# Stores of values in plain patterns, a gathered load, and bias sums queued behind other GpSimd work, in a two-network transformer kernel

## The chip, the cores and the metric

The kernel runs on one core of a Trainium2 chip. Its time is the device time of one execution in microseconds (us); the time of record is the median of several executions. A profiled execution of the same kernel gives the trace from which all rows below are read. The engines are named as the profile names them: PE (TensorE matmul), PEld (its weight load), DVE (VectorE), ACT (ScalarE), POOL (GpSimd) and SP (SyncE, which here only issues DMAs). A name such as SPq or POOLq is the queue of DMAs that this engine issues.

## The reference, cut to what matters

Two networks of two layers each work on 512 tokens of width 1024, in fp32. Each layer of the first network projects its input once and feeds three attention branches:

```
proj = h @ w_in[l]
c_q, c_kv, k_r, qkv_b, qkv_c, gate_logits = jnp.split(proj, IN_SPLITS, axis=-1)
y_a = mla_mixer(c_q, c_kv, k_r, ...)          # latent attention, 8 heads
y_b = dilated_mixer(q_b, k_b, v_b)            # DIL_PATTERNS = ((128,1),(512,4),(2048,16)), 4 heads each
y_c = neighbourhood_mixer(q_c, k_c, v_c, rpb) # 8 heads on an 8 x 64 grid, a learned bias
merged = sum of gates[i] * (y_i @ w_i);  x = x + merged @ w_o;  then a gated feed-forward block
```

The dilated branch splits the 512 tokens into 1, 4 or 16 interleaved sequences and lets each head attend within its own sequence. With dilation 16, token t belongs to sequence t mod 16, and each sequence holds 32 tokens. The neighbourhood branch lets each grid cell attend to a window of 8 x 16 cells, with a bias added to the scores. The second network (attention, short convolution, Fourier mixing) isn't touched by the change.

## The kernel before, in words

Each fp32 product is made as three matmuls of split operands (a high and a low part), so every weight tile is loaded by SP into `wst`, split by ACT into `whi` (line 251) and by DVE into `wlo` (line 252), and used by PE in lines 269 to 271. Tokens are in the columns of most tiles; the values of the dilated and neighbourhood branches are the exception.

`v_tokens` computes these values with tokens in the rows, for 5 units of 4 heads: units 0 and 1 together, then unit 2 (the third dilated group), then units 3 and 4 (the two neighbourhood groups). For each block of 128 tokens (`tk`), ACT and DVE split the product into the tile `vn` (lines 254 and 255, two buffers), and `v_store` sends it by one GpSimd DMA (line 759) to the DRAM tensor `vd` of 512 rows and 2560 columns. Unit 0 and 1 are stored with rows in the order of the tokens. Unit 2 is stored with its rows sorted by sequence (row 32 r + l for token 16 l + r) and units 3 and 4 with theirs sorted by grid column. The sorting is done by the DRAM side of the store: its pattern has an outer level of 8 (unit 2) or 2 (units 3 and 4), a second level of 16 or 64, and rows of 512 columns. `v_load` reads the values back by GpSimd DMAs (line 769) into a tile `V`, one pair of heads at a time, when the unit needs them; for unit 2 that is one DMA of rows in storage order.

`branches` puts the groups of attention heads into one stream: latent attention, three dilated groups, two neighbourhood groups. `attn_pair` handles a pair of heads as steps of three parts: `score` (line 341; a mask or a bias is added by DVE in line 348), `turn` (a transpose by PE in line 365, and its split) and `value` (lines 392 or 406). `stream` issues the score of a step, then the turn of the step before it, then the value of the step before that; dense products fill the spaces between (`weave`). In its last lines `value` adds three parts of the output: ACT copies two, DVE adds (line 416), GpSimd adds the last (line 417).

For a pair of neighbourhood heads, `pre` loads the bias of each of the two heads from DRAM on the GpSimd queue (line 1015) into a tile `bias` (two buffers) and adds the constant mask `maskc` on GpSimd (line 1016). `maskc` is loaded by SP into the space that `krhl` held; `krhl` is last read by the DMAs of line 860. `dil_merge` weights the three dilated groups: it stores statistics by line 516, reads them back (line 963), computes on DVE, stores and reads back factors (lines 979 and 521), and multiplies (line 984, DVE).

The softmax denominators of the other groups go a like way: `inverse` copies a row (line 508, DVE), stores it (line 510), reads it back spread over 64 partitions (line 521), and DVE multiplies by it (line 877).

Nothing fixes the order of instructions on an engine by hand, but for a few places with `issue_after`, which puts an instruction behind a given one on the same engine without a wait on data. A planner orders each engine's instructions as the program is built: it simulates engines and DMAs with its own costs, and takes the foremost instruction of the program that it believes ready. On the chip each engine then works in that order, and an instruction that waits holds all behind it.

Of the kernel before, what the change touches and what calls it, by code (L numbers as in the profile page):

```python
# [11 lines left out]
F32 = mybir.dt.float32  # L12
F32R = mybir.dt.float32r
AF = mybir.ActivationFunctionType
ALU = mybir.AluOpType
# [6 lines left out]
P = 128  # L22
# [192 lines left out]
class _Net:  # L215
# [105 lines left out]
    def attn_pair(self, scores, nk, mask, v, order, rq=None, wide=False, pre=None, post=None, home=None):  # L321
# [5 lines left out]
        nc = self.nc  # L327
# [51 lines left out]
        def value(j, g):  # L379
            rows = slice(64 * j, 64 * j + 64)  # L380
            o = c["o"]
            cost = 0
            if wide:
                if g == 0:
                    c["ob"] = self.bank("O")
                ob = c["ob"]
                if g % 2:
                    qs = slice((g - 1) * P, (g + 1) * P)
                    ph, pl = c.pop(("p", j, g // 2))
                    for x in (ph, pl):  # L390
                        for kt in range(nkt):
                            self.last = nc.tensor.matmul(ob[:, qs], v(j, 0, kt), x[:, kt], start=x is ph and kt == 0,  # L392
                                                         stop=x is pl and kt == nkt - 1)
                            cost += 110
                if g == 3:
                    nc.scalar.activation(o[rows], ob[64:128], AF.Copy)
                    nc.vector.tensor_tensor(o[rows], ob[0:64], o[rows], op=ALU.add)
            else:

                p = c.pop(("p", j, g))  # L400
                for hb in range(per // 2):
                    ob = self.bank("T" if hb else "O")
                    b0 = g * per + 2 * hb
                    for i in range(2):
                        for kt in range(nkt):
                            nc.tensor.matmul(ob[:, i * 256:i * 256 + 256], v(j, b0 + i, kt),
                                             p[:, (2 * hb + i) * nkt + kt].rearrange("p a q -> p (a q)"),
                                             start=kt == 0, stop=kt == nkt - 1)
                            cost += 110
                    dst = self.two_blocks(order(o[rows]), b0)  # L410
                    part = lambda r, x: self.two_parts(ob[r], x, dst)
                    ll = self.t(self.tp, "ll", (P, 256), bufs=2)
                    lo = self.two_blocks(ll[rows], 0, like=dst)
                    nc.scalar.activation(lo, part(slice(0, 64), 1), AF.Copy)
                    nc.scalar.activation(dst, part(slice(64, 128), 0), AF.Copy)
                    nc.vector.tensor_tensor(dst, part(slice(0, 64), 0), dst, op=ALU.add)  # L416
                    nc.gpsimd.tensor_tensor(dst, dst, lo, op=ALU.add)  # L417
            if g == 4 // per - 1 and j == 1 and post:
                c["late"](o)
            return cost  # L420

        steps = [(lambda j=j, g=g: score(j, g), lambda j=j, g=g: turn(j, g), lambda j=j, g=g: value(j, g))
                 for j in range(2) for g in range(4 // per)]
        return [(pre if i == 0 else None, *s) for i, s in enumerate(steps)]
# [297 lines left out]
    def v_tokens(self, win, rc, vd):  # L722

        sl = [slice(tk * P, (tk + 1) * P) for tk in range(4)]
        w = 2560
        at = lambda o, *ap: bass.AP(vd.tensor, vd.offset + o, [list(x) for x in ap])
        ps = [self.bank(x) for x in ("mm", "mm", "mm", "T")]
        for k in range(8):  # L730
            if k % 2 == 0:
                wt = self.weights(win[24 + k // 2])
            o = slice(k % 2 * 512, k % 2 * 512 + 512)
            for tk in range(4):
                self.mm3(ps[tk], self.hh[:, k, sl[tk]], self.hl[:, k, sl[tk]], wt[0][:, o], wt[1][:, o], k == 0, k == 7)
                yield 650
        for tk in range(4):
            self.v_store(ps[tk], rc()[:, tk:tk + 1], vd[sl[tk], 0:1024], "p" + "hl"[tk % 2])
        for u in (2, 3, 4):
            wt = [self.weights(win[24 + 2 * u + c]) for c in range(2)]  # L740
            for tk in range(4):
                if tk % 2 == 0:
                    bk = self.bank("mm")
                ps = bk[:, tk % 2 * 256:tk % 2 * 256 + 256]
                for k in range(8):
                    o = slice(k % 4 * 256, k % 4 * 256 + 256)
                    self.mm3(ps, self.hh[:, k, sl[tk]], self.hl[:, k, sl[tk]], wt[k // 4][0][:, o], wt[k // 4][1][:, o],
                             k == 0, k == 7)
                    yield 330
                dst = at(8 * tk * w + 512 * u, (w, 8), (32 * w, 16), (1, 512)) if u == 2 else \  # L750
                    at(2 * tk * w + 512 * u, (w, 2), (8 * w, 64), (1, 512))
                self.v_store(ps, rc()[:, tk:tk + 1], dst, "vn")
        yield 0

    def v_store(self, ps, scale, dst, tag):
        n = ps.shape[1] // 64
        vn = self.t(self.tp, tag, (P, n, 2, 64), F32R, bufs=2)
        self.split(vn[:, :, 0], vn[:, :, 1], ps.rearrange("p (h d) -> p h d", h=n), scale)
        self.nc.gpsimd.dma_start(out=dst, in_=vn.rearrange("p h x d -> p (h x d)").bitcast(F32))

    def v_load(self, vd, pair, width, parts):

# [9 lines left out]
    def branches(self, l, r, put_r, gates, first_outputs, first_products, load_split, qk_tiles, qc):  # L772
        nc, a = self.nc, self.a
        h = (self.hh, self.hl)
        nat = lambda ap: ap
        win = a["win"][l]
        rows = lambda j: slice(64 * j, 64 * j + 64)

        def const(src, n, name, tag=None):
            c = self.cp.tile([P, n], F32, name=f"{name}{l}", tag=tag or name)  # L780
            nc.sync.dma_start(out=c, in_=src)
            return c


        st = {}
# [86 lines left out]
        def finish(i, order, tap, stay=False):  # L872
            def f(stats):
                rd = self.inverse(stats[:, 1])

                def late(o):
                    nc.vector.tensor_tensor(order(o), order(o), self.blocked(rd, order), op=ALU.mult)
                    self.tap(*tap[:1], o, tap[1])
                    if not stay:
                        self.put_y(i, o)  # L880
                        return
                    x = qk_tiles()
                    self.split(x[:, 0], x[:, 1], o)
                    qc[0].append(x[:, 0])
                    qc[1].append(x[:, 1])
                return late
            return f
# [11 lines left out]
        def unit(u, put, vparts, res):  # L899
            for p in range(2):  # L900
                q, *ks = [qk_tiles() for _ in range(3)]
                t = [q[:, 0], q[:, 1]] + [x[:, i] for i in range(2) for x in ks]
                for side in range(2):
# [6 lines left out]
        orders = (nat, lambda ap: ap.rearrange("p (l r) -> p r l", r=4), lambda ap: ap.rearrange("p (l r) -> p r l", r=16))  # L910
        vparts = ([(0, [(1, P)], (P, 4), 0), (4, [(1, P)], (P, 3), 64)],
                  [(0, [(4, P)], (1, 4), 0)],
                  [(0, [(1, P)], (P, 4), 0)])
        g0tiles = ((0, 1), (4, 5), (5, 6), (2, 3))
        g0keys = (0, 64, 192, 256)
        sd = self.t(self.dr, "sd", (6, 4, S), bufs=1)
# [86 lines left out]
        def nb_groups(u):  # L1003
            if u == 0:
                st["mc"] = const(a["maskC"], 768, "maskc", "krhl")
            groups = []
            for p in range(2):
                t, v = res["C", u][p]
                bias = {}

                def pre(bias=bias, p=p):
                    for j in range(2):
                        bt = self.t(self.tp, "bias", (P, 768), bufs=2)
                        hd = 4 * u + 2 * p + j
                        nc.gpsimd.dma_start(out=bt, in_=a["rpb"][l, hd])
                        nc.gpsimd.tensor_tensor(bt, bt, st["mc"], op=ALU.add)
                        bias[j] = bt
                    return iter(())
                groups += self.attn_pair(
                    self.pair_scores(t, bs, lambda x, b: x[:, 8 * KC0[b]:8 * KC0[b] + 256]), 256,  # L1020
                    lambda j, b, bias=bias: bias[j][:, CTYPE[b] * 256:CTYPE[b] * 256 + 256],
                    lambda j, b, kt, v=v: v[:, g0tiles[b][kt], j * P:(j + 1) * P], blk, pre=pre,
                    post=finish(6 + 2 * u + p, blk, (f"yc{l}", (2 * u + p) * P), u == 1))
            return groups
# [646 lines left out]
```

## Time and profile before

| | us |
|---|---|
| median of 3 runs | 2438.22 (2437.87 to 2441.62) |
| profiled execution, its own time | 2432.9 |
| its span in the trace | 2431.1 |
| PE busy in the span | 2325.6 |
| DVE busy | 1571.2 |
| ACT busy | 1169.5 |
| POOL busy | 695.4 |

The profiled execution took 1.8 us more than its span in the trace, and 5.3 us less than the median of the runs. PE is busy in 96% of the span. The two layers of the first network hold the stages that the change touches: from about 50 to 450 us in the first layer and from about 985 to 1450 us in the second. The granted TensorE clock is 0.984 of full speed over the span.

### The profile page before, as it was taken

How to read it: one execution, taken by the hardware profiler on the slowest of the kernel's cores; microseconds unless marked ns; L12 is line 12 of the kernel's file. 1: busy time of each engine (PE TensorE's matmuls, PEld its weight loads, DVE VectorE, ACT ScalarE, POOL GpSimd, SP SyncE). 2: the span in 40 equal slices, each digit the busy share in tenths (PEclk: the TensorE clock that was granted, in tenths of full speed). 3: DMA queues.
4: the chain of work that ended last, by engine and by line, in shares of the span. 5: the costliest groups of instructions: out<-in, count | busy, mean ns of one | idle time of the engine just before them, and what ended most of it. 6: DMA issues, size and time to landing. Idle time of an engine off the chain costs nothing. (4 is left out here: it accounts for less than half of the span.)

```text
span 2431.1 us, 31714 instructions
## 1 busy us (share of the span) xinstructions
PE 2325.6 (96%) x11356; PEld 1932.1 (79%) x11356; DVE 1571.2 (65%) x2367; ACT 1169.5 (48%) x2064; POOL 695.4 (29%) x745
## 2 busy tenths in 40 slices
PE   8989999989999999989999999999999899979996
PEld 7878887878888888878887877878877788858884
DVE  6768798665443334857788656777333767697666
ACT  5656685434222223646676444323222466435653
POOL 3135456332111001223356423111112121242215
PEclk9999999999999999999999999999999999989998
DMA  5445457555333344544546656876344332324222
GB/s 185 136 152 156 146 165 229 183 183 173 95 96 98 104 130 141 147 142 127 166 138 205 224 162 197 275 257 200 95 133 139 115 96 82 92 77 124 75 82 78
DMA packets 135405, 352.62 MB, mean 145 GB/s; under 512 B 26552, under 2 KB 33944, under 8 KB 135248
## 3 DMA queue, kind: packets, MB, share of 16 engines
q1 hardware_dynamic: 103760, 279.91, 35.9%
q0 software_dynamic: 31488, 70.69, 10.1%
q8 instruction: 89, 1.46, 0.3%
q14 instruction: 68, 0.56, 0.1%
HBM read 281.54 MB, written 41.66 MB: 133 GB/s over the span
## 5 line engine op out<-in xcount | busy, mean ns | idle before, releaser
L251 ACT ACTIVATE whi<-wst 128x1024 fp32r<-128x1024 f32 (+4 forms) x387 | 374.0, 967 | 626.4 <-PE mm L270 187.5
L252 DVE TENSOR_TENSOR wlo<-wst,whi 128x1024 fp32r<-128x1024 f32 (+4 forms) x387 | 471.4, 1219 | 257.4 <-ACT whi L251 256.7
L271 PE MATMUL mm<-hh,wlo 128*128 128x512 f32 x1184 | 467.1, 395 | 8.2 <-DVE wlo L252 8.2
L269 PE MATMUL mm<-hh,whi 128*128 128x512 f32 x1184 | 473.0, 400 | 0.5 <-ACT tmp L538 0.5
L270 PE MATMUL mm<-hl,whi 128*128 128x512 f32 x1184 | 466.6, 394 | 0.0
L271 PEld LDWEIGHTS mm<-hh,wlo 128*128 128x128 f32 x1184 | 223.8, 189 | 55.9 <-DVE wlo L252 9.0
L269 PEld LDWEIGHTS mm<-hh,whi 128*128 128x128 f32 x1184 | 224.2, 189 | 41.0 <-ACT tmp L538 0.7
L270 PEld LDWEIGHTS mm<-hl,whi 128*128 128x128 f32 x1184 | 224.3, 189 | 40.7 <-issue 0.2
L706 POOL TENSOR_TENSOR s<-s,rf 128x512 f32<-128x512 f32 x44 | 75.9, 1726 | 398.0 <-ACT s L705 398.0
L541 POOL DMA_DIRECT2D ry<-tmp x136 | 67.9, 505 | 184.8 <-ACT tmp L538 86.6
L341 PE MATMUL S<-qk,qk 128*128 128x512 f32 (+2 forms) x512 | 108.1, 329 | 12.2 <-ACT E L353 12.2
L365 PE MATMUL T<-ident,E 128*128 128x128 f32 x768 | 117.1, 273 | 1.0 <-ACT E L353 1.0
L251 ACT ACTIVATE ph<-T 128x512 fp32r<-128x512 f32 x160 | 94.6, 595 | 45.5 <-PE T L365 43.8
L365 PEld LDWEIGHTS T<-ident,E 128*128 128x128 f32 x768 | 94.0, 141 | 19.1 <-ACT E L353 1.2
L252 DVE TENSOR_TENSOR pl<-T,ph 128x512 fp32r<-128x512 f32 x128 | 87.2, 683 | 25.6 <-ACT ph L251 25.1
L341 PEld LDWEIGHTS S<-qk,qk 128*128 128x128 f32 x512 | 79.8, 192 | 23.7 <-ACT E L353 14.6
L350 ACT ACTIVATE E<-E,stats 128x256 f32<-128x256 f32 (+1 forms) x160 | 73.0, 457 | 51.9 <-DVE stats L348 51.4
L417 POOL TENSOR_TENSOR O<-O,ll 64x256 f32<-64x256 f32 x72 | 75.1, 1045 | 65.7 <-DVE O L416 61.3
L303 POOL TENSOR_TENSOR tmp<-tmp,tmp 128x512 f32<-128x512 f32 x26 | 41.7, 1603 | 170.5 <-ACT tmp L299 166.6
L269 PE MATMUL S<-hh,whi 128*128 128x512 f32 x208 | 82.3, 395 | 6.0 <-ACT hh L254 6.0
L271 PE MATMUL S<-hh,wlo 128*128 128x512 f32 x208 | 82.0, 394 | 1.5 <-DVE wlo L252 1.5
L270 PE MATMUL S<-hl,whi 128*128 128x512 f32 x208 | 82.1, 395 | 0.0
(649 smaller groups left out, 5491.5 us busy)
## 6 DMA issues: line engine op xcount, KB each, us to landing
wst<-win SPq DMA_DIRECT2D x153, 512.0 KB, 3.8
wst<-w SPq DMA_DIRECT2D x120, 512.0 KB, 3.6
mw<-wada SPq DMA_DIRECT2D x48, 512.0 KB, 4.4
td<-gate SPq DMA_DIRECT2D x48, 256.0 KB, 3.5
V<-vd POOLq DMA_DIRECT2D x20, 512.0 KB, 5.4
qk<-qk POOLq DMA_DIRECT2D x40, 256.0 KB, 4.0
ry<-tmp POOLq DMA_DIRECT2D x136, 64.0 KB, 3.8
wst<-wo SPq DMA_DIRECT2D x16, 512.0 KB, 3.8
```

What stands on the lines that cost most here:

```text
L251: nc.scalar.activation(hi, src, AF.Copy)
L252: nc.vector.tensor_tensor(lo, src, hi.bitcast(F32), op=ALU.subtract)
L269: mm(out, ah, bh, start=start, stop=False, **kw)
L270: mm(out, ah, bl, start=False, stop=False, **kw)
L271: mm(out, al, bh, start=False, stop=stop, **kw)
L303: self.nc.gpsimd.tensor_tensor(new, acc, sq, op=ALU.add)
L341: nc.tensor.matmul(sp[:, i * nk:(i + 1) * nk], a, b, start=n == 0, stop=n == len(ops) - 1)
L350: nc.scalar.activation(e[:, sl], e[:, sl], AF.Exp, scale=-1.0, bias=m, accum_out=d)
L365: nc.tensor.transpose(tp[:, i * P:(i + 1) * P], e[:, i * P:(i + 1) * P], self.ident)
L417: nc.gpsimd.tensor_tensor(dst, dst, lo, op=ALU.add)
L541: nc.gpsimd.dma_start(out=y[r:r + 32], in_=f[r ^ 32:(r ^ 32) + 32])
L706: nc.gpsimd.tensor_tensor(s, s, r, op=ALU.mult)
```

## The change

There are three parts.

1. Stores. `v_store` takes a list of (rows of the tile, DRAM pattern) and issues one DMA for each. Unit 2 is now stored in the order of the tokens (one DMA for 128 rows, as before). For units 3 and 4 each store becomes two, of 64 rows each, with one row stride.
2. Load. Unit 2's `V` is gathered on loading: for each pair of heads four DMAs of 128 rows (4 sequences of 32 tokens each) take the place of one of 512 rows.
3. Bias sums. `value` keeps its last GpSimd addition (line 417) as `self.summed`, and the addition of bias and mask (line 1016) is queued behind the one kept at that point of the program.

```diff
@@ attn_pair, value
-                    nc.gpsimd.tensor_tensor(dst, dst, lo, op=ALU.add)
+                    self.summed = nc.gpsimd.tensor_tensor(dst, dst, lo, op=ALU.add)
@@ v_tokens
-            self.v_store(ps[tk], rc()[:, tk:tk + 1], vd[sl[tk], 0:1024], "p" + "hl"[tk % 2])
+            self.v_store(ps[tk], rc()[:, tk:tk + 1], [(slice(0, P), vd[sl[tk], 0:1024])], "p" + "hl"[tk % 2])
...
-                dst = at(8 * tk * w + 512 * u, (w, 8), (32 * w, 16), (1, 512)) if u == 2 else \
-                    at(2 * tk * w + 512 * u, (w, 2), (8 * w, 64), (1, 512))
+                dst = [(slice(0, P), vd[sl[tk], 1024:1536])] if u == 2 else \
+                    [(slice(64 * i, 64 * i + 64), at((2 * tk + i) * w + 512 * u, (8 * w, 64), (1, 512))) for i in range(2)]
@@ v_store
-        self.nc.gpsimd.dma_start(out=dst, in_=vn.rearrange("p h x d -> p (h x d)").bitcast(F32))
+        for rows, d in dst:
+            self.nc.gpsimd.dma_start(out=d, in_=vn[rows].rearrange("p h x d -> p (h x d)").bitcast(F32))
@@ branches
-                  [(0, [(1, P)], (P, 4), 0)])
+                  [(0, [(1, 4), (16, 32)], (4, 4), 0)])
@@ nb_groups, pre
-                        nc.gpsimd.tensor_tensor(bt, bt, st["mc"], op=ALU.add)
+                        with self.tc.issue_after(self.summed.ins):
+                            nc.gpsimd.tensor_tensor(bt, bt, st["mc"], op=ALU.add)
```

## Rows read from the trace of the kernel before

**Rows 1.** The page: busy us and share of each engine.
```profile
PE 2325.6 (96%) x11356; PEld 1932.1 (79%) x11356; DVE 1571.2 (65%) x2367; ACT 1169.5 (48%) x2064; POOL 695.4 (29%) x745
```

**Rows 2.** Timeline, first layer: start, length, engine, line, operation, idle before and releaser.
```profile
133.05 0.47 DVE L255 SCALAR_TENSOR_TENSOR vn<-mm,rc,vn 128x256 fp32r<-128x256 f32 x1
...
138.00 4.63 POOL L1016 TENSOR_TENSOR bias<-bias,maskc 128x768 f32<-128x768 f32 x2 [9.78 <-DMA maskc<-maskC]
142.59 1.63 POOL L759 DMA_DIRECT2D vd<-vn  x2
...
154.32 0.47 ACT L254 ACTIVATE vn<-mm,rc 128x256 fp32r<-128x256 f32 x1 [9.72 <-DMA vd<-vn]
...
157.21 1.65 PE L341 MATMUL S<-qk,qk 128*128 128x512 f32 x3 [6.58 <-ACT E L353]
```

**Rows 3.** Windows behind two stalls: busy of PE, PEld, DVE, ACT, POOL; PEclk, DMA, GB/s.
```profile
157.20:162.00 4.80, 4.79 (x17) 4.38 (x18) 3.69 (x6) 2.34 (x6) 2.12 (x3) 0.51 0.91 292
...
1090.60:1094.00 3.40, 3.34 (x9) 2.70 (x10) 3.40 (x7) 1.78 (x4) 0.84 (x1) 0.53 0.74 254
```

**Rows 4.** Timeline, second layer, same columns as rows 2.
```profile
1069.54 0.27 DVE L508 COPY row<-T 8x128 f32<-8x128 f32 x1
...
1069.80 3.65 POOL L1016 TENSOR_TENSOR bias<-bias,maskc 128x768 f32<-128x768 f32 x2 [12.95 <-DMA maskc<-maskC]
1073.39 1.67 POOL L759 DMA_DIRECT2D vd<-vn  x2
...
1085.24 1.09 POOL L521 DMA_DIRECT2D RD<-rdd  x2 [9.64 <-DMA rdd<-row]
...
1088.78 0.69 DVE L877 TENSOR_TENSOR O<-O,RD 128x512 f32<-128x512 f32 x1 [10.87 <-DMA RD<-rdd]
...
1090.66 0.80 PE L271 MATMUL mm<-hh,wlo 128*128 128x512 f32 x1 [8.24 <-DVE wlo L252]
```

**Rows 5.** Second layer: two PE waits (timeline), ACT's waits from 980 to 1130.
```profile
1045.30 0.96 PE L341 MATMUL S<-qk,qk 128*128 128x512 f32 x3 [1.23 <-ACT E L353]
...
1053.97 0.39 PE L269 MATMUL mm<-whi,hh 128*128 128x256 f32 x1 [0.73 <-DVE vn L255]
...
ACT vn L254 <- DMA vd<-vn: 8.7, 2, 5.0
```

**Rows 6.** Line 759, units 3 and 4, second layer: issue ns and landing us, min/median/max.
```profile
L759 POOL DMA_DIRECT2D vd<-vn x8: 801/837/852, 1020.8 to 1092.5; - x8
...
DMA to landing us min/median/max: 8.5/10.2/12.5
```

**Rows 7.** Line 759, unit 2, second layer.
```profile
DMA to landing us min/median/max: 4.3/4.6/5.0
```

**Rows 8.** Line 759, units 0 and 1, second layer (512 KB each).
```profile
L759 POOL DMA_DIRECT2D vd<-ph x2: 532/574/617, 989.0 to 990.3; - x2
...
DMA to landing us min/median/max: 3.4/5.5/7.7
```

**Rows 9.** Timeline, first layer, where the neighbourhood group begins.
```profile
343.84 1.70 POOL L417 TENSOR_TENSOR O<-O,ll 64x256 f32<-64x256 f32 x2
344.30 0.41 DVE L348 CUSTOM_DVE_ANT_0 E<-S,bias 128x256 f32<-128x256 f32 x1
...
347.86 0.60 POOL L516 DMA_DIRECT2D sd<-row  x1 [2.32 <-DVE row L515]
```

**Rows 10.** Timeline, first layer, the merge of the dilated groups.
```profile
376.53 0.69 DVE L984 TENSOR_TENSOR o<-o,RD 128x512 f32<-128x512 f32 x1 [4.61 <-DMA RD<-fd]
...
377.76 1.22 PE L406 MATMUL O<-pl,V 128*128 128x256 f32 x4 [3.37 <-DVE O L416]
```

**Rows 11.** First layer: unit 2's first load of values, and the first addition after its use.
```profile
305.12 0.80 POOL L769 DMA_DIRECT2D V<-vd  x1
...
336.41 0.90 POOL L417 TENSOR_TENSOR O<-O,ll 64x256 f32<-64x256 f32 x1 [0.56 <-DVE O L416]
...
L769 POOL DMA_DIRECT2D V<-vd x2: 802/808/814, 305.1 to 327.0; - x2
```

## The prediction, made before the changed kernel was run

> **What bounds the kernel now.** The page comes first: PE is busy for 2325.6 of 2431.1 us [rows 1], so only some 105 us can be won without taking work from PE, and every edit here is worth what it does to PE's idle time and to its clock. Next I asked for busy time and granted clock in stretches of 10 us through the two layers of the first network, to find where PE stands still. Three places lie where values are stored or a bias sum runs; at each, the timelines of POOL, ACT, DVE and PE side by side tell what it waits for.
>
> First place, first layer, 150.6 to 157.2 us. PE waits 6.58 us for an exponential on ACT. ACT is late because its split of the last value tile waits 9.72 us for a free buffer of `vn`, that is for a store of values to land. That store was issued at 142.59, though its tile was complete at 133.5. What held it is the pair of bias sums in front of it on POOL: they waited 9.78 us for the mask to land and then ran 4.63 us [rows 2]. Nothing needs these sums before 344.30 [rows 9]. After the stall PE runs for 4.8 us at a granted clock of 0.51, so near 1.2 instead of 2.4 GHz [rows 3].
>
> Second place, second layer, 1082.4 to 1090.7 us. PE waits 8.24 us for a low weight part. DVE could not make it, since it stood 10.87 us at a multiplication by a denominator that hadn't landed. POOL read it back only at 1085.24, after 9.64 us of waiting for a stored row of 4 KB. That row was ready at 1069.81 and was issued at about 1075.06, behind two bias sums (again held, 12.95 us, by the mask) and two value stores [rows 4]. So the row lost 5.25 us before it was issued and some 10 us in landing, behind two stores that themselves land in about 10 us [rows 6]. The clock stays at 0.53 for 3.4 us after it [rows 3].
>
> Third place, second layer, 1044 to 1054 us: PE waits 1.23 and 0.73 us. ACT waited for `vn` buffers there as well, 8.7 us in two waits [rows 5].
>
> **The stores.** All 128-row stores of `vn` carry 256 KB; only the DRAM pattern differs. With an outer level of 2 (units 3 and 4) they take 8.5 to 12.5 us to land [rows 6], with an outer level of 8 (unit 2) 4.3 to 5.0 [rows 7]. The stores of units 0 and 1, plain rows, land in 3.4 to 7.7 us with twice the bytes [rows 8]. The row stride doesn't explain it, for unit 2's was the longest. So I expect the new halves (64 rows, 128 KB, plain) to land in 3 to 5 us and bound them by 3.4 and 10.2. Unit 2 gains at most a microsecond, on a landing that nobody waits for.
>
> The Trainium skill says the same in "DMA: Bandwidth & Descriptors", section "Why a DMA increments its semaphore by 16 and not by 1": a transfer runs on the largest number of engines, at most 16, that divides the outer counts of both patterns, so 2, then 8, then 16 here; the trace agrees in order (10.2, 4.6 and 5.5 us). It also speaks against a part of the change: the gathered loads have an outer count of 4, so 4 engines each, and if that made them late enough to reach PE by the 10 us worked out below, in one layer, the gain would be 6.8 instead of 16.8 us.
>
> On POOL each store of units 3 and 4 becomes two issues. One cost 0.837 us [rows 6]; a plain one costs 0.574 [rows 8]. That is +0.31 us for each of 16, about 5 us of POOL over the kernel, beside 71% of idle time [rows 1].
>
> **The gathered load.** Four issues of about 0.808 us take the place of one, +2.4 us for each of four loads, 9.7 us of POOL in all [rows 11]. The first load is issued at 305.12, and the addition that follows its use comes at 336.41, so there are about 31 us for it [rows 11]. With an outer count of 4 I bound one gathered DMA by the landings for counts 8 and 2, 4.6 and 10.2 us, at half the bytes of either. Four in a row at 4.6 are 18 us and hidden; four at 10.2 would be 41 us and 10 too late. I take it as hidden, since halving the bytes puts each nearer the lower end.
>
> **The bias sums.** The sums now stand behind the addition of line 417 that was traced last. A score is traced two steps ahead of its value, so for the first neighbourhood pair that is the second addition of the pair issued at 343.84, which ends at 345.54 [rows 9]. POOL no longer stands at 128 or 1057 us, so the value stores and the row go out when they are ready. This has two prices.
>
> One is the mask on DVE: the first use of a bias was at 344.30, and the first sum (1.83 us, half of 3.65 [rows 4]) can end at 347.4 at the earliest, so DVE is held 3.1 us unless the planner puts other work before it. At the merge DVE stood 4.61 us and PE, which stopped 2.47 us later, lost 3.37 [rows 10]. So about 2.5 us of a hold on DVE are free; 3.1 cost 0.6 us a layer, 1.2 in all. For later pairs I count nothing here and leave them to rival (c).
>
> The other is the merge. Its store of statistics stands at 347.86 [rows 9]. With two sums of 1.83 us from 345.54 it goes out at 349.2, 1.35 us late. The merge's end already stops PE for 3.37 us [rows 10], so this passes through: 2.7 us in two layers. The bounds are 0 (the planner lets the store go first) and 3.7 us a layer.
>
> **The sum.** First place: 6.58 us, and 4.8 x (1 - 0.51) = 2.35 us for the clock, 8.9. Second place: 8.24 + 3.4 x (1 - 0.53) = 9.8. Third place: 1.23 + 0.73 = 2.0. Together 20.7 us. Less 1.2 for the masks and 2.7 for the merge it is 16.8. From the profiled execution's 2432.9 us that is 2416.1; this execution lies 5.3 us under the median, so against the median of 2438.22 I predict 2421.
>
> What comes next where the stalls go: at the first place ACT reaches the same order 9.72 us sooner where PE waited 6.58, so 3 us are left [rows 2]. At the second the row would be issued near 1071 behind the same stores, land with them near 1075, be read back by about 1080 (1085.24 to 1088.78 is 3.5 us [rows 4]), and the weight part (1.9 us from 1088.78 to 1090.66) would be ready near 1081, with 1 to 2 us to spare before 1082.4. That is the tightest step.
>
> **Rivals.** (a) The stores land no sooner, because two halves of one tile share what limited the whole. Then only the hold is lifted. The first place still goes (the store is issued 9.1 us earlier, and ACT waited 9.72). At the second, 5.25 of 8.24 us go and the clock stays low. Gain 8.9 + 5.2 less 3.9, or 10.2: 2428. For it: the halves go out together. Against it: rows 6 to 8, where only the outer count differs. The Trainium skill's page "DMA: Bandwidth & Descriptors", section "Rules for kernel authors", holds that two transfers to disjoint partition halves run one after the other; that rule would lean to this case. No row of this trace shows two such halves.
>
> (b) POOL's new order costs more than I took: both sums pass whole into the merge (3.7 us a layer) and the mask's hold whole into PE (3.1). That is 13.6 us of the 20.7: gain 7.1, 2431. For it: the sums stand ahead of the merge in the program, and the planner takes the foremost. Against it: 2.5 us of slack at the merge [rows 10].
>
> (c) Slower. If each of the eight pair starts held DVE for 3.1 us and PE felt all of it, that would be 24.8 us, with 2.7 for the merge 27.5 against 20.7: 2445. It decides once a hold costs PE more than 2.25 us (20.7 - 2.7 over 8), so with under a microsecond of slack on DVE. The merge shows 2.5.
>
> (d) The planner makes the order anew, and the merge's stall (3.37 us and a slow clock after it, about 5 us a layer) goes as well in both layers: 2411.
>
> (e) The change doesn't do what it says: the planner had placed the sums late in its own view and the edge alters nothing. Excluded here, since in the first layer they were issued some 200 us ahead of their first use [rows 2, 9].
>
> **How the numbers follow.** The forecast has 0.60 (its own range 2415 to 2427, from the bounds of the merge and the third place), (a) 0.10, (b) 0.12, (c) 0.06, (d) 0.12. The range from 2411 to 2431 takes in (a), (b) and (d) at their prices and leaves out (c) and the tails. A change within 0.2%, 4.9 us, can't be told from none in this kernel: under 2433.3 is faster, over 2443.1 slower. Part of (b) and the better part of (c) fall inside: faster 0.88, same 0.06, slower 0.06.
>
> **What would show it.** In the changed profile: no bias sum on POOL before about 340 and 1275 us; landings of units 3 and 4 of 3 to 5 us; no wait of ACT for `vn`; PE busy throughout 150 to 160 and 1080 to 1090 at full clock; a hold on DVE of up to 3 us at the first neighbourhood mask; the merge's stall 1 to 2 us longer. Wrong would be: landings that stay near 10 us, or new PE idle time over 5 us a layer from 340 to 430 and from 1275 to 1360 us.

## The result, and the profile after

The changed kernel takes 2409.86 us (median of 4 runs, 2409.14 to 2413.86), the kernel before 2439.86 on the same chip (4 runs, 2437.87 to 2441.62): a ratio of 0.9881, 95% interval 0.9864 to 0.9898, so 25 to 33 us less. I had forecast 2421 in a range of 2411 to 2431. The direction was right; the gain was underestimated, and the time lies just under the range.

The two profiled executions differ by less, 2432.9 against 2413.86 us. The one of before was faster than all 60 runs of that kernel beside the experiments (2434.05 to 2449.39), and the one of after the slowest of its four. With a second profile of either (runs e4 and e3 below) the spans are 2435.6 and 2408.6 us, 27.0 apart.

The page after, its span and its busy line, against [rows 1]:

```profile
span 2412.1 us, 31728 instructions
...
PE 2323.6 (96%) x11356; PEld 1930.6 (80%) x11356; DVE 1576.2 (65%) x2367; ACT 1169.7 (48%) x2064; POOL 707.0 (29%) x773
```

PE does the same work. GpSimd has 28 instructions and 12 us more; the two value stages below show no wait for them.

The stores of units 3 and 4 in the second layer, with the last of unit 2 (line 760 after; issue in ns, landing in us, as in [rows 6]):

```profile
L760 POOL DMA_DIRECT2D vd<-vn x17: 527/535/569, 1010.9 to 1071.0; - x17
...
DMA to landing us min/median/max: 2.2/2.9/5.1
```

Half of a tile lands in 2.9 us where a whole one took 10.2 [rows 6]; in the first layer it lands in 3.1 us (2.2 to 6.7) where a whole one took 10.5 (9.0 to 11.7). ACT's wait for a `vn` buffer, 8.7 us in two waits before [rows 5], isn't among its waits any more.

The two value stages after, as windows (length, busy us of PE, PEld, DVE, ACT and POOL with their counts, granted clock of PE, DMA share, GB/s):

```profile
100.00:200.00 100.00, 100.00 (x614) 88.49 (x613) 74.86 (x123) 65.26 (x129) 31.69 (x54) 1.00 0.50 145
900.00:1130.00 230.00, 229.77 (x1279) 198.97 (x1278) 160.66 (x238) 126.40 (x225) 62.33 (x92) 1.00 0.48 148
```

PE idles 0.23 us in 330, at full clock. The row of 4 KB that was read back after 9.64 us of waiting [rows 4] is now read back after 2.66, and in the first layer after 5.58 where it was 10.47 (GpSimd's timeline after, both layers):

```profile
137.47 0.52 POOL L510 DMA_DIRECT2D rdd<-row  x1 [1.07 <-DVE row L508]
143.57 1.08 POOL L521 DMA_DIRECT2D RD<-rdd  x2 [5.58 <-DMA rdd<-row]
...
1059.76 0.52 POOL L510 DMA_DIRECT2D rdd<-row  x1
1062.94 1.08 POOL L521 DMA_DIRECT2D RD<-rdd  x2 [2.66 <-DMA rdd<-row]
```

The start of the neighbourhood group and the merge after, first layer, against [rows 9, 10] (GpSimd's, DVE's and PE's timelines):

```profile
335.63 3.66 POOL L1018 TENSOR_TENSOR bias<-bias,maskc 128x768 f32<-128x768 f32 x2
...
337.51 0.42 DVE L348 CUSTOM_DVE_ANT_0 E<-S,bias 128x256 f32<-128x256 f32 x1 [0.95 <-POOL bias L1018]
...
339.25 0.61 POOL L516 DMA_DIRECT2D sd<-row  x1
...
365.81 0.69 DVE L985 TENSOR_TENSOR o<-o,RD 128x512 f32<-128x512 f32 x1 [4.78 <-DMA RD<-fd]
...
367.05 0.74 PE L406 MATMUL O<-pl,V 128*128 128x256 f32 x4 [2.15 <-DVE O L416]
```

The sums have moved to 335.63 us, in the second layer to 1254.86. DVE is held by the first of them for 0.95 us, in the second layer for 1.01. The merge's stall stays, as DVE's wait of 4.78 us (4.61 before).

### The profile page after: what moved, and what is told of

It is laid out like the page before. It is cut to its first block, busy times and chain, and to the rows that moved or that the text cites. A ratio compares the mean times of both kernels' runs of the same rounds, so it can differ in the third digit from the quotient of the medians.

```text
span 2412.1 us, 31728 instructions
## 1 busy us (share of the span) xinstructions
PE 2323.6 (96%) x11356; PEld 1930.6 (80%) x11356; DVE 1576.2 (65%) x2367; ACT 1169.7 (48%) x2064; POOL 707.0 (29%) x773
## 3 DMA queue, kind: packets, MB, share of 16 engines
q0 software_dynamic: 25792, 70.65, 10.2%
## 5 line engine op out<-in xcount | busy, mean ns | idle before, releaser
L252 DVE TENSOR_TENSOR wlo<-wst,whi 128x1024 fp32r<-128x1024 f32 (+4 forms) x387 | 481.7, 1245 | 255.5 <-ACT whi L251 255.1
L252 DVE TENSOR_TENSOR pl<-T,ph 128x512 fp32r<-128x512 f32 x128 | 87.4, 684 | 27.1 <-ACT ph L251 26.5
```

Of the source, the lines that this page charges most:

```text
L252: nc.vector.tensor_tensor(lo, src, hi.bitcast(F32), op=ALU.subtract)
```

## The experiments

### First group: the change taken apart

**e1, the edge alone.** The kernel before, with this and nothing else:

```diff
-                    nc.gpsimd.tensor_tensor(dst, dst, lo, op=ALU.add)
+                    self.summed = nc.gpsimd.tensor_tensor(dst, dst, lo, op=ALU.add)
...
-                        nc.gpsimd.tensor_tensor(bt, bt, st["mc"], op=ALU.add)
+                        with self.tc.issue_after(self.summed.ins):
+                            nc.gpsimd.tensor_tensor(bt, bt, st["mc"], op=ALU.add)
```

> The kernel before with the bias sums queued behind the kept addition, stores and loads as before. Theory (two causes add up: the hold of GpSimd by the early bias sums, and value stores that land in about 10 us because their DRAM pattern has an outer level of 2): the stall at 150 us in the first layer goes (9 us with its slow clock), the stall near 1082 us shrinks from 8.2 to about 3 us, the small waits near 1045 stay, landings stay at 8.5 to 12.5 us; 10 us under before in all, 2430 where before has 2440. Rival 1 (only the hold matters): the whole 30 us, 2410. Rival 2 (only the landing matters): within 3 us of before.

**e2, the stores alone.** The changed kernel without these lines.

> The kernel before with the new stores and the gathered load, bias sums placed freely by the planner. Theory (two causes): landings of units 3 and 4 near 3 us, GpSimd still held for about 10 us by the sums in both layers. The stall at 150 us becomes about 2 us or none (the store is issued at 142.6 and lands at 146 instead of 154), the one near 1082 shrinks to about 2 us, the waits near 1045 go; 18 us under before, 2422. Rival 1 (only the hold matters): within 5 us of before. Rival 2 (only the landing matters): all 30 us, 2410.

**e3 and e4.** The changed kernel and the kernel before once more, beside the other two.

> The changed kernel once more, for a second trace and more times. Theory (the profiled execution of before was 7 us faster than its other runs, the one of after 4 us slower, so the traces show 19 us of a 30 us difference): median near 2410, profiled execution anywhere from 2408 to 2414. Rival (30 us was chance of few runs, the real difference is the 17 forecast): median near 2420.

> The kernel before once more, for a second trace. Theory (the three stalls in the value stage vary with the landing of slow stores from execution to execution, and were short in the first trace): median near 2440; if this profiled execution is nearer the median, its extra time lies in the stalls near 150 and 1040 to 1100 us. Rival (the spread lies elsewhere, in stages that the change doesn't touch): extra time in other windows, or none in this trace.

Measured, all on one chip: e1 2428.90 (ratio 0.9953, 0.994 to 0.9965), e2 2411.34 (0.988, 0.9866 to 0.9894), e3 2410.02 (0.9877, 0.9863 to 0.989), e4 2437.51 (0.9995, 0.9984 to 1.0005). The two value stages of e4, e1 and e2, as windows like those above:

```profile
100.00:200.00 100.00, 92.11 (x553) 81.10 (x552) 67.24 (x104) 57.04 (x113) 29.90 (x43) 0.97 0.45 134
900.00:1130.00 230.00, 217.78 (x1170) 186.93 (x1169) 138.06 (x202) 109.94 (x192) 46.78 (x59) 0.97 0.45 136
```

```profile
100.00:200.00 100.00, 93.54 (x557) 81.94 (x556) 67.15 (x106) 57.48 (x115) 26.86 (x42) 0.97 0.46 138
900.00:1130.00 230.00, 221.74 (x1204) 190.03 (x1203) 143.90 (x209) 113.19 (x200) 48.07 (x65) 0.99 0.47 141
```

```profile
100.00:200.00 100.00, 99.95 (x611) 88.06 (x610) 74.63 (x123) 64.64 (x129) 35.60 (x56) 1.00 0.50 145
900.00:1130.00 230.00, 229.76 (x1279) 198.87 (x1278) 162.79 (x238) 125.96 (x224) 65.72 (x94) 1.00 0.48 148
```

PE idles 20.1 us in e4 (7.89 and 12.22), 14.7 in e1 and 0.3 in e2. The edge alone helps, by 11.5 us (2440.45 less 2428.90), near the 10 of its theory, but that is partly luck: of the 9 us that the theory had in the first layer it wins 1.4 us of idle time (7.89 to 6.46). The stores alone do all that the whole change does, within 1.3 us: my theory of two causes that add up (2422 for e2) is wrong, and its rival (2410) right. e3's theory held. For e4 the rival did: its profiled execution is 4.4 us longer than the first one of before, and the extra time doesn't lie in the value stages (the table further down).

The edge alone leaves a stall at the first place, though no sum stands there any more. Its GpSimd, DVE and PE timelines:

```profile
138.29 0.55 POOL L510 DMA_DIRECT2D rdd<-row  x1 [0.75 <-DVE row L508]
151.04 1.09 POOL L521 DMA_DIRECT2D RD<-rdd  x2 [12.20 <-DMA rdd<-row]
...
155.76 0.69 DVE L877 TENSOR_TENSOR O<-O,RD 128x512 f32<-128x512 f32 x1 [4.18 <-DMA RD<-rdd]
...
157.98 0.80 PE L341 MATMUL S<-qk,qk 128*128 128x512 f32 x1 [4.57 <-ACT E L353]
```

The row of 4 KB goes out at 138.29 with nothing computed ahead of it, and still takes 12.2 us to be read back, behind stores that land slowly.

Why is the hold by the mask harmless in e2? I looked for what the mask's own load waits for, and found it in the second layer. The waits of SyncE's queue from 1030 to 1075 us in the kernel before (us in total, times, longest):

```profile
SPq L781 <- DMA qk<-krhl: 16.9, 2, 10.8
```

GpSimd's and SyncE's timelines there, in the kernel before and then in e2:

```profile
1048.38 1.08 POOL L521 DMA_DIRECT2D RD<-rdd  x2 [10.17 <-DMA rdd<-row]
1049.46 0.52 POOL L860 DMA_DIRECT2D qk<-krhl  x1
...
1056.31 0.54 POOL L860 DMA_DIRECT2D qk<-krhl  x1
...
1066.66 0.33 SPq L781 DMA_DIRECT2D maskc<-maskC  x1
```

```profile
1049.77 0.33 SPq L782 DMA_DIRECT2D maskc<-maskC  x1
...
1052.90 4.11 POOL L1017 TENSOR_TENSOR bias<-bias,maskc 128x768 f32<-128x768 f32 x2 [0.51 <-DMA maskc<-maskC]
```

The mask takes over the buffer of `krhl`, so its load waits until both copies out of `krhl` have landed. GpSimd issues these copies, behind the value stores, and behind an earlier row that came back after 10.17 us. So in the second layer the mask was late because the stores were slow: the 12.95 us of [rows 4] were their effect, and no second cause beside them. With quick stores the mask's load is issued 67.2 us after the layer's first value store (at 982.6) where it was 77.7 (at 989.0 [rows 8]), and the sums are held 0.51 us. In the first layer e2 still holds them 8.52 us (at 132.52, until the mask lands), and the stores behind them, which land in 6.5 to 7.0 us where they took 11.3 to 11.7, are early enough all the same.

### Second group: is it the pattern, the queue or the buffers?

**e5.** The kernel before with

```diff
-                dst = at(8 * tk * w + 512 * u, (w, 8), (32 * w, 16), (1, 512)) if u == 2 else \
-                    at(2 * tk * w + 512 * u, (w, 2), (8 * w, 64), (1, 512))
+                dst = at(8 * tk * w + 512 * u, (w, 8), (32 * w, 16), (1, 512))
```

> The kernel before with one edit: the neighbourhood units' values are stored in the pattern that the third dilated unit's stores had (8 runs of 16 rows where there were 2 of 64), still in one transfer each and with the old gathering of sums. The values come to stand in other rows, so the neighbourhood branch multiplies other values than the reference's; the work is the same. Theory, the pattern of the store alone sets the stall: these stores land in about 4.6 us where they took 10.2, the statistics row queued behind them lands in about 5 us less, and the kernel takes 2414 (2410 to 2418). Rival, what helped was that each store became two transfers, or that its copy was taken plainly: landings stay above 8 us and the time within 3 us of before's 2438.

Measured: 2416.95 (ratio 0.9889, 0.9869 to 0.9909), as its theory had it. Its stores from 1012 us on, and its value stages:

```profile
L758 POOL DMA_DIRECT2D vd<-vn x9: 601/632/652, 1012.3 to 1072.9; - x9
...
DMA to landing us min/median/max: 4.0/5.1/6.7
```

```profile
100.00:200.00 100.00, 100.00 (x614) 88.42 (x613) 74.80 (x122) 65.03 (x131) 33.04 (x50) 1.00 0.49 145
900.00:1130.00 230.00, 229.77 (x1277) 198.82 (x1276) 161.31 (x236) 124.85 (x223) 59.92 (x81) 1.00 0.50 147
```

Still one transfer of 128 rows, still the edge missing, and the whole loss in the value stages is gone. So it was the pattern with its outer level of 2, and neither the cutting in two nor the edge was needed for it. The edit changes the length of a run (16 rows for 64) and the row stride along with the outer level; the halves of the change keep the old stride and the 64 rows and land fast, so these two are not what was slow.

**e7 and e8.** The kernel before, with the stores of units 2 to 4 (e7) or the row of reciprocals (e8) given to SyncE's queue:

```diff
-        self.nc.gpsimd.dma_start(out=dst, in_=vn.rearrange("p h x d -> p (h x d)").bitcast(F32))
+        (self.nc.sync if tag == "vn" else self.nc.gpsimd).dma_start(out=dst, in_=vn.rearrange("p h x d -> p (h x d)").bitcast(F32))
```

```diff
+            plain = len(dst.shape) == 2
...
-            nc.gpsimd.dma_start(out=dst, in_=row)
+            (nc.sync if plain else nc.gpsimd).dma_start(out=dst, in_=row)
```

> The kernel before with one edit: the stores of all three 256-wide units go through SyncE's queue and not GpSimd's, patterns as they were. The order on TensorE, VectorE and ScalarE is that of before. Theory, the stall comes from the slow landing in GpSimd's queue, where a 4 KB row then waits behind it: with the stores elsewhere the row lands in about 3 us, the value stages lose under 3 us each instead of 10 and 16, and the kernel takes 2413 (2409 to 2420; upwards if SyncE's weight loads wait behind a store's copy). Rival, the pattern is slow on any queue and what counts is that a copy's buffer comes free: ScalarE's wait for vn stays and the time is 2428 or more.

> The kernel before with one edit: the row of reciprocals, which GpSimd's queue stored behind the values, is stored from SyncE's queue; values and sums as before. Theory, the row queued behind the slow stores is the larger of the two ways in which they reach TensorE (the other is ScalarE's wait for a copy's buffer, 8.7 us in two places): the first layer's stall and most of the second's go, 2422 (2417 to 2430). Rival, the buffers are the larger way: within 5 us of before. Other rival, SyncE's weight loads wait behind the row: slower than before.

Measured: e7 2429.90 (0.995, 0.9933 to 0.9968), e8 2437.65 (0.9985, 0.9972 to 0.9998). Both theories missed. The number of e7's rival came out, but not its mechanism, since ACT's wait for `vn` is gone; in e8 the first rival, the buffers, fits best. On this chip before took 2442.69 us, so e7 won 12.8 us and e8 5.0, where e5 won 25.7. ACT's waits in e7 from 40 to 180 us, and its first value stage:

```profile
ACT whi L251 <- DMA wst<-win: 8.4, 1, 8.4
```

```profile
100.00:200.00 100.00, 92.21 (x554) 80.85 (x554) 67.54 (x105) 56.63 (x113) 24.96 (x37) 0.97 0.43 135
```

ACT's waits in e8 over the same stretch, and the reading back of the row in its DMA issues (count, KB each, median us to landing):

```profile
ACT vn L254 <- DMA vd<-vn: 15.4, 3, 9.7
```

```profile
RD<-rdd POOLq DMA_DIRECT2D x4, 128.0 KB, 8.1
```

In e7 ACT no longer waits for a buffer of `vn`, but once for 8.4 us for a weight, whose loads now share SyncE's queue with the stores. In e8 the row leaves the slow queue, yet it is read back through that queue, in 8.1 us (2.9 before), and ACT waits for `vn` longer than before. The slow stores reach PE by three ways at once, the row, the buffers and the mask; shutting one hands part of the loss to another.

**e6 and e11.** The changed kernel, with unit 2 stored and loaded as before (e6), or with four transfers of 32 rows for each store of units 3 and 4 (e11):

```diff
+                dst = [(slice(0, P), at(8 * tk * w + 512 * u, (w, 8), (32 * w, 16), (1, 512)))] if u == 2 else \
...
+                  [(0, [(1, P)], (P, 4), 0)])
```

```diff
+                    [(slice(32 * i, 32 * i + 32), at((2 * tk + i // 2 + i % 2 * 256) * w + 512 * u, (8 * w, 32), (1, 512))) for i in range(4)]
```

> The changed kernel with one part undone: the third dilated unit's values are stored in 8 runs of 16 rows and loaded in one transfer, as before. Theory: its stores landed in 4.6 us before and nothing waited for them, and the four loads by 2.8 us of issue lay ahead of their use, so this part is worth nothing: 2410 (2407 to 2413). Rival, the part has a share in the gain: 2413 or more. Other rival, its six more DMA issues on GpSimd cost: 2407 or less.

> The changed kernel with each store of a neighbourhood unit's values cut into four transfers of 32 rows where it has two of 64: 16 more DMA issues in a layer, some 0.54 us of GpSimd each. Theory, the number of transfers does not matter as long as each goes row by row: within 3 us of the changed kernel, 2410. Rival, a transfer has a fixed price in the queue, and a row queued behind four lands later: 2414 or more.

Measured: e6 2408.19 (0.9859, 0.9837 to 0.988), e11 2413.47 (0.9885, 0.9869 to 0.9901); both intervals overlap that of the changed kernel. Unit 2's part shows no gain here. e11's time lies between its theory (2413 at most) and its rival (2414 or more), so a small price for more transfers isn't excluded; they land no later than the halves:

```profile
L760 POOL DMA_DIRECT2D vd<-vn x33: 496/498/577, 1009.2 to 1069.6; - x33
...
DMA to landing us min/median/max: 1.9/2.7/4.6
```

### Third group: the merge, and a faster version

**e9 and e10.** The changed kernel with the merge's six products on GpSimd (e9), or the first three of them (e10, `(nc.vector if p else nc.gpsimd)` in the same line):

```diff
-                    nc.vector.tensor_tensor(outs[g, p], outs[g, p], f, op=ALU.mult)
+                    nc.gpsimd.tensor_tensor(outs[g, p], outs[g, p], f, op=ALU.mult)
```

> The changed kernel with one edit: the six products of the dilated merge in each layer are made by GpSimd, which then waits for the spread weights in VectorE's place. Theory, what is left of the stalls around the merge comes from VectorE's wait for that transfer: in the changed kernel TensorE loses 5.0 us to idle time and slow clock from 350 to 390 us and 5.6 us from 1270 to 1310 us, and most of it goes: 2402 (2399 to 2406). Rival, GpSimd's wait and its six products hold back the sums of bias and mask and the output sums behind them, and VectorE waits for those: 2410 or more.

> The changed kernel with the merge's first three products of each layer on GpSimd, the last three on VectorE. Theory: the first product has the long wait (4.8 us), so most of the same gain with half of the work on GpSimd: 2403 (2400 to 2407). Rival, VectorE meets the later products' transfers in the same way, since GpSimd issues them only behind its own products: 2408 to 2413.

Measured: e9 2394.32 (0.9806, 0.9792 to 0.9819), e10 2411.37 (0.9875, 0.9861 to 0.9889). e9 won more than its theory had (2399 to 2406), e10 nothing, as its rival had it. The windows around the two merges, of the changed kernel first, then e9:

```profile
350.00:410.00 60.00, 56.36 (x277) 46.53 (x276) 50.69 (x88) 35.92 (x76) 39.19 (x46) 0.97 0.68 216
1265.00:1325.00 60.00, 55.67 (x278) 46.08 (x278) 50.37 (x93) 34.03 (x70) 38.37 (x46) 0.97 0.68 205
```

```profile
350.00:410.00 60.00, 59.45 (x301) 49.41 (x300) 51.21 (x85) 38.77 (x83) 47.93 (x52) 1.00 0.69 220
1265.00:1325.00 60.00, 59.21 (x298) 48.95 (x297) 49.60 (x80) 36.84 (x76) 49.82 (x54) 1.00 0.70 217
```

PE's idle time falls from 7.97 to 1.34 us and the clock stays full: with 3% of 112 us for the clock that is 10 us at the place of the edit. The other 6 of the 16 lie in no single place that I found. In e9 VectorE waits 3.9 us for a bias sum that now stands behind the products, as its rival had feared, but PE idles only 0.55 us in that window. e10 clears most of the same windows (3.4 us of idle time are left), and gives the time back behind the first merge:

```profile
400.00:410.00 10.00, 7.72 (x38) 5.95 (x36) 9.97 (x15) 4.18 (x9) 8.23 (x7) 1.00 0.21 68
...
420.00:430.00 10.00, 8.73 (x33) 6.79 (x34) 7.76 (x14) 5.26 (x12) 2.84 (x3) 0.83 0.52 180
```

**e12 to e16.** The same edit on e6 (e12), on e2 (e13), on the kernel before (e14), and e9 and e13 again on one chip (e15, e16).

> The kernel that took 2394 (the changed one with the merge's products on GpSimd), with the third dilated unit stored in 8 runs of 16 rows and loaded in one transfer, as before the change. Theory, that unit's part of the change is worth nothing: 2394 (2391 to 2397). Rival, it has a share in the gain: 2397 or more. Other rival, its extra issues cost: 2391 or less.

> The same kernel of 2394 with the edge of the sums of bias and mask taken away, so that GpSimd waits some 8 to 12 us for the mask in the value stages again. Theory, with fast landings that hold is covered and the edge is worth 0 to 2 us: 2395 (2393 to 2398). Rival, with fewer stalls elsewhere the hold shows: 2400 or more.

> The kernel before with one edit, the merge's products on GpSimd. Theory, the stalls of the merge and those of the value stages are independent: 16 us less than before, 2425 (2421 to 2429). Rival, part of those 16 us was won only because the value stages were free of stalls: 2430 or more.

> The changed kernel with the merge's products on GpSimd once more, on the same chip as the one beside it. Theory, its 2394 is its own and not that chip's: 2394 (2391 to 2397). Rival, the chip gave part of it: 2400 or more.

> The same without the edge on the sums of bias and mask, which took 2404 on another chip, on the same chip as the one beside it. Theory, the difference of 9 us between the two belongs to the kernels, whose orders of work differ in many places and not only at the sums: 2403 (2400 to 2406). Rival, it was the chip: within 3 us of the one beside it.

Measured: e12 2404.12 (0.9852, 0.9831 to 0.9872), e13 2403.68 (0.9842, 0.9829 to 0.9855), e14 2432.35 (0.9958, 0.9945 to 0.9971), e15 2397.21 (0.9799, 0.978 to 0.9817), e16 2404.83 (0.9836, 0.982 to 0.9851). Of these theories only e16's held; e15's was missed by 0.2 us, and in e12, e13 and e14 the number of the rival came out. On one chip, then, the edge is worth 7.6 us in this kernel (e15, e16). It isn't the mechanism of e13's rival: the hold shows nowhere at the sums' place, and from 100 to 200 and from 900 to 1130 us PE loses at most 0.23 us with the edge or without. Some 3 us of it lie in the first layer between the last value store and the first addition of line 669, where the gated branches are summed (358.7 and 359.3 us with the edge, 362.1 and 362.0 without). PE's order of work differs between the two from the first layer's attention on, since the planner makes it anew; whether the edge gains by itself or by that order stays open. For unit 2's part, e12 lies 6.9 us above e15, the kernel of e9 on the same chip, and the difference shows at the merge. PE idles 6.1 us in e12's windows around the two merges, with a clock of 0.97, and 1.1 us in e15's, at full clock:

```profile
350.00:410.00 60.00, 56.61 (x280) 47.10 (x279) 47.96 (x81) 34.75 (x72) 44.62 (x51) 0.97 0.70 211
1265.00:1325.00 60.00, 57.30 (x284) 47.64 (x283) 48.49 (x84) 36.17 (x73) 42.86 (x50) 0.97 0.69 207
```

So with unit 2 as before, moving the products shows no gain (e6 0.9859, e12 0.9852). PE's order of work differs here too, and what of it is unit 2's part stays open. In e14 the merge's edit gives 10.7 us, not the 16 of its theory but the 10.6 that I had read from the windows, while the value stages lose what they did:

```profile
100.00:200.00 100.00, 91.50 (x552) 80.44 (x551) 67.35 (x104) 56.96 (x113) 29.96 (x43) 0.97 0.46 134
900.00:1130.00 230.00, 216.03 (x1176) 184.45 (x1175) 141.33 (x206) 110.18 (x194) 50.12 (x66) 0.99 0.46 136
```

So the merge's stall can be taken away with the slow stores in place as well as without them: PE idles 1.6 us around the two merges in e14 and 7.6 in before. e9 (2394 and 2397 on two chips) is the fastest version found.

## What the prediction had right, and the step that failed

**Right.** The stores' pattern as cause; landings of 3 to 5 us (medians 2.9 and 3.1, in the first layer up to 6.7); ACT's wait for `vn` gone; PE busy throughout at both places (10.00 of 10 us from 150 to 160 and from 1080 to 1090); a hold on DVE at the first mask of under 3 us (0.95 and 1.01); the gathered loads hidden (each lands in 5.2 us, 4.6 to 6.2).

**The step that failed is the sum.** Two of its terms were mis-sized, both towards a smaller gain: it took three places for the whole loss of the value stages (20.7 us, where 28.9 were lost), and it charged 3.9 us for masks and merge, which were not paid. These windows of the kernel before, the value stages and the merges, can be set against those of the changed kernel above:

```profile
100.00:200.00 100.00, 91.39 (x550) 80.45 (x549) 66.59 (x103) 56.20 (x112) 30.39 (x44) 0.97 0.46 134
900.00:1130.00 230.00, 216.06 (x1175) 184.48 (x1174) 140.26 (x204) 111.27 (x195) 49.41 (x64) 0.99 0.45 136
350.00:410.00 60.00, 56.63 (x277) 46.87 (x276) 51.58 (x93) 36.10 (x77) 37.77 (x47) 0.94 0.66 209
1265.00:1325.00 60.00, 55.78 (x276) 45.94 (x275) 49.88 (x95) 40.57 (x87) 29.29 (x39) 0.94 0.59 181
```

The time from one matmul to another can also be compared. PE has the same 11356 matmuls before and after, and their order differs in 126 places, all of them in the stretches of masks and merges. Numbered from 0 by their start, they give (us; e4 and e3 are the second profiles of before and after):

| | before | after | e4 | e3 |
|---|---|---|---|---|
| value stages (matmuls 459 to 1007 and 4585 to 5406) | 250.0 | 221.1 | 249.7 | 221.1 |
| masks and merge (1007 to 2211 and 5406 to 6752) | 510.1 | 508.1 | 513.6 | 507.6 |
| the rest of the span | 1671.0 | 1682.9 | 1672.3 | 1680.0 |

First, the three places. I summed the long waits that I had singled out, 16.8 us of idle time and 3.9 for the clock. In the profile of before PE idles 8.6 us from 100 to 200 and 13.9 from 900 to 1130, 22.5 in all; with the clock, in stretches of 10 us, it loses 26.5, and 0.2 after. The clock's term was right (4.0). What I left out were waits of 0.3 to 1.6 us around the three places, 5.7 us in sum, which belong to the same slow stores, since e5 clears them by the pattern alone. Matmul to matmul the two stages are 28.9 us shorter (28.6 from e4 to e3), and they take 221.1 us in e5, e6 and e9 too. I had taken the hold by the mask for a cause beside the stores, and so looked at the places where it ended; e2 and the mask's own load show it was in part their effect.

Second, the price at mask and merge, 3.9 us. The hold of 0.95 us on DVE stopped PE nowhere. At the merge PE's idle time from 350 to 410 and 1265 to 1325 us is 7.97 us; before it was 7.59, by its waits for line 416. The clock there rose from 0.94 to 0.97, and with it, in stretches of 10 us, the two merges lose 10.7 us after and 13.3 before. The store of statistics comes after the sums, as I thought, but the merge then waits for the same transfer as before. So no price shows. The expectation that this stall grows by 1 to 2 us a layer is wrong: PE's longest wait there went from 3.37 to 2.15 us in the first layer, with a new one of 1.5 for ACT. By the table masks and merge are even 2.0 and 6.0 us shorter; but before and e4, one program, differ there by 3.5, so a gain isn't shown.

The rest of the span, for which the sum had no term, is 11.9 and 7.7 us longer in these pairs, 2.8 and 2.7 of it after the last matmul; its cause stays open. From e4 to e3, whose times lie near the medians, the spans differ by 26.9 us where I had 16.8: 7.9 more in the value stages, 9.9 more at masks and merge, 7.7 less in the rest. Setting the gain, read from one execution, against the median did no harm, since the value stages of e4 are no longer than those of before.

**The rivals.** (a) is refuted: two halves land in 2.9 us. The Trainium skill's rule on two partition halves ("DMA: Bandwidth & Descriptors", section "Rules for kernel authors": they run one after the other, so one transfer of 128 partitions is to be used) doesn't decide here, since two halves beat the one transfer by far, and four quarters land no later. The Trainium skill's other rule, in "Why a DMA increments its semaphore by 16 and not by 1" of the same page, agrees once more: an outer level of 8 in place of 2 took the landing from 10.2 to 5.1 us (e5). No run shows how many engines a transfer used. (b) and (c) are refuted by the hold of 0.95 us and the merge. (d) has nearly the measured time, 2411, but by luck: the idle time of the merge's stall is still there, and only 2.6 of the 10 us that (d) gives it are gone. The range's lower end had come from (d) alone; the bounds of the main terms didn't reach so far, because I had bounded the costs but not the idle time itself.

## What to carry to other kernels

Before costing single stalls, take PE's idle time and clock over the whole stage that shares a resource: the small waits around a long one can have its cause, and here they were a quarter of the idle time. When a wait for a load looks like a cause of its own, ask which buffer that load takes over and who has to release it; here the trail led back to the same slow stores. A small transfer came late here behind stores that land slowly in the same queue (a row of 4 KB after 9.64 us). Moving it to another queue won 5.0 us and moving the slow transfers 12.8, since part of the wait was handed on; mending their pattern won 25.7.

## What was unexpected

The pattern on the DRAM side sets a store's landing: with an outer level of 2 it is 10.2 us for 256 KB, with 8 it is 5.1 for the same bytes in the same queue (e5), and plain halves and quarters take 2.9 and 2.7 (after, e11). GpSimd's products of 128x512 took a median of 1.29 us where VectorE's took 0.69 (e9, after), and were still the better choice there by some 15 us: the wait for their operand then stands in GpSimd's order, where PE hardly feels it. That is no general rule, since in e12 the same move gained nothing that shows.
